# S5 layers on four quarters of the TensorE array, and the first layer's rotation tables from ScalarE sines

## The chip, the core and the metric

The kernel runs on one core of one Trainium2 chip. A core has engines that run side by side and are ordered only by semaphores: TensorE (PE in the profile; its weight loads are PEld), VectorE (DVE), ScalarE (ACT), GpSimd (POOL) and SyncE (SP), which issues transfers; ScalarE and POOL issue transfers too, each from its own queue. The metric is the device time of one execution in microseconds, median of the runs; lower is better.

## The reference

A trunk of four pre-norm residual layers over 256 positions of width 1024, one sequence. Layer i has the mixer i mod 3, so layers 0 and 3 are S5, layer 1 is forgetting attention, layer 2 gated linear attention. Every layer then has a squared-ReLU MLP (width 4096) and a gated per-layer input. What the change touches is the S5 mixer:

```python
def s5_mixer(xn, w_in, lam_re, lam_im, log_dt, b_re, b_im, c_re, c_im, d_skip, w_glu, w_out):
    u = xn @ w_in                                   # 64 groups of 16 channels, 64 states each
    dt = exp(log_dt)[:, None]
    mag = exp(lam_re * dt)
    ab_re, ab_im = mag * cos(lam_im * dt), mag * sin(lam_im * dt)
    ...                                             # bbar = coef(ab, lam) * b
    # per chunk: x = u . bbar (complex); s_t = ab * s_(t-1) + x_t; y = Re(s . c)
    ...
    y = y + d_skip * u
    z1, z2 = split(gelu(y) @ w_glu, 2)
    return (z1 * sigmoid(z2)) @ w_out
...
for i in range(DEPTH):
    h = h + mixer_i(rmsnorm(h, norm_mix[i]))
    h = h + square(relu(rmsnorm(h, norm_mlp[i]) @ mlp_w1[i])) @ mlp_w2[i]
    h = h + (p[i] @ ple_proj[i]) * sigmoid(rmsnorm(h, norm_ple[i]) @ ple_gate[i])
return rmsnorm(h, final_norm)
```

## The kernel before

Activations are kept transposed (channels on partitions, time along the row) in four tiles of 128 x 2 x 256. Large weights come in units of 256 x 512 (512 KB) through three `raw` buffers; ScalarE rounds each unit to a high part (`whi`, line 182), VectorE forms the rest (`wlo`, line 184), and TensorE does three (or, for the wide MLP products, effectively one and a half) passes with them. This is the work of most of the span.

An S5 layer is cut into four blocks b = 0 to 3 of 16 groups. A block's 16 groups stand as 8 pairs p; pair member g = 0 or 1 lies on the lower or the upper 64 partitions. Time is cut into 64 steps of 4 positions: the way in gathers 4 positions x 16 channels = 64 rows into 64 states, a scan runs over the 64 steps, and the outputs take 64 states back to 4 x 16 rows. A complex state is turned by a rotation table (`rot`, 128 x 8 x 2 x 64) so that the scan has a real factor only, and turned back behind it.

The work is written as steps with one letter and the block's number, and two orders by hand, `FIRST` for layer 0 and `LATER` for layer 3, say in which order the steps are traced. The tile framework then orders each engine's instructions by that priority and by when it expects them to be ready; in layer 3 TensorE's order is pinned to the traced one, and a short head of layer 0 (up to `u0`) is pinned on ScalarE, TensorE and, at its end, VectorE. The steps that matter here:

- `w` / `u`: half a block of the dense input product (line 1241), then its scaling by the row scale (line 1247) and eight small transfers that gather `U` (line 1075, four from SP's queue, four from ScalarE's). `z0`, `z1`: the row scale (POOL's power, line 365; TensorE and ScalarE, lines 375 and 377).
- `f`: loads of the way-in weights; in layer 0 of their parts, and `i` forms them on VectorE (lines 968 to 970); in layer 3 of the finished weights (one buffer, `win`) and the finished rotation table.
- `r`: block b's rotation table in layer 0, on VectorE: two products of 128 x 1024 (line 990) and two sums of 128 x 512 (lines 992, 993) from `F1` and `F8`, tables of powers that `s5_scalars` forms at the start with some fifty short complex products (lines 879 to 903, helper lines 783 to 785). `rot` for block 0 is begun in the head, between `z1` and `u0`.
- `o`, `k`: output weights (lines 1008 to 1012) and the short-range kernel (lines 1033 to 1044), which goes through memory into `tm` (line 1052).
- `x`: the way in, on TensorE (line 1087). `s`: states on VectorE (two products of 128 x 1024 at line 1097, two sums at 1098 and 1099, two scans at 1102). `e`: turned back (lines 1112 to 1121). `y`: outputs on TensorE (line 1133), Gelu on ScalarE (line 1142). `t`, `g`: transposed and split (lines 1149, 1150, 1313).
- `P`, `p`: the layer's input projection (line 470). `d`, `l`: loads and splits of gate weights (the second half of `w_glu`), `a`, `b`: the gate products for them (lines 201 to 203). These are dense work put between the S5 steps.

In layers 0 to 2, `s5_ahead` prepares layer 3's tables a little at a time behind the MLP and leaves them in memory (`kept`).

The way in and the outputs work on 64 x 64 pieces, and both pair members stay on their own half of the array:

```python
for g in range(2):
    r = slice(g * 64, (g + 1) * 64)
    matmul(px[r, p, :], w[r, p], U[r, p, :], ...)   # rows of half g, columns of half g
```

PSUM tiles come from tags: `wk` (3 buffers), `acc` (3), `mk` (1) and `po` (1); the outputs of a block go to `mk`, the transposes of `t` to `po`, which `g` reads.

Of the kernel before, what the change touches and what calls it, by code (L numbers as in the profile page):

```python
# [9 lines left out]
F32 = mybir.dt.float32  # L10
# [12 lines left out]
        "acc": 3, "wk": 3, "po": 1, "mk": 1}  # L23
# [37 lines left out]
class Trunk:  # L61


    def __init__(self, ctx, tc, A):
# [45 lines left out]
        nc.gpsimd.memset(self.halfpi, math.pi / 2)  # L110
        self.tms = [const(f"tm{i}", [P, 8, 4, 16]) for i in range(3)]
# [680 lines left out]
    def s5_scalars(self, j, late=False):  # L792
# [81 lines left out]

        F1, by_pair = self.small("F1", [128, 2, 32, 8], bufs=1), self.small("F8", [128, 32, 2, 8], bufs=1)
# [27 lines left out]
        d = self.small("dd", [128, 8, 16], bufs=1)  # L903
        self.tc.keep_in_program_order(V.tensor_tensor(d, self.eye16.unsqueeze(1).broadcast_to([128, 8, 16]), sd.unsqueeze(2).broadcast_to([128, 8, 16]), ALU.mult))
        r4 = new("r4")
        tt(r4, mag, mag, ALU.mult)
        tt(r4, r4, r4, ALU.mult)
        q = dict(cpow=G, powers=F, r4=r4, F1=F1, F8=by_pair, d=d)
        return q

    def s5_table(self, j, F):
# [9 lines left out]
        tab = self.dram.tile([2, 4, 4, 2, 8, 64], F32, name=f"tab{j}")  # L921
        for i in range(2):
            for g in range(2):
                nc.gpsimd.dma_start(tab[g, :, :, i].rearrange("s b p n -> (s b) p n"), ct[:, i, g, :])
        return tab

    def s5_spread(self, b):

        out = []
        for i in range(2):  # L930
            ps = self.psum()
            for p in range(8):
                for g in range(2):
                    self.last_mm = self.nc.tensor.matmul(ps[g * 64:(g + 1) * 64, p * 64:(p + 1) * 64], self.pick[:, p], self.ct[:, i, g, :], start=True, stop=True, skip_group_check=True)
            out.append(ps)
        return out
# [8 lines left out]
    def s5_fetch_in(self, j, b, pin=lambda x: x):  # L945
        bT = self.t4("bT", (128, 2, 512), tag="wt")
        pin(self.nc.gpsimd.dma_start(bT, self.A["s5_bT"][j, b]))
        return bT

    def s5_fetch_powers(self, tab, b, pin=lambda x: x):  # L950
        cf = self.t4("coef", (128, 2, 512), tag="wt")
        for g in range(2):
            pin(self.nc.gpsimd.dma_start(cf[g * 64:(g + 1) * 64], tab[g, :, b].rearrange("s i p n -> s (i p n)").unsqueeze(0).broadcast_to([16, 4, 1024])))
        return cf
# [6 lines left out]
    def s5_in(self, b, bT, cf, ahead=False):  # L961

        nc = self.nc
        if not ahead:
            w = [self.wp.tile([128, 2, 8, 64], F32, name=n, tag=n, bufs=BUFS[n]) for n in ("wh", "wl")]
            f = [t.rearrange("x i p n -> x i (p n)") for t in w]
            re, im = cf
            nc.vector.tensor_tensor(f[0], bT, re.unsqueeze(1).broadcast_to([128, 2, 512]), ALU.mult)
# [4 lines left out]
        w = [self.flat(win[:, i]) for i in range(2)]  # L973
        t = self.scratch((2, 512))
        t = [t[:, i] for i in range(2)]
        self.two(w[0], bT[:, 0], cf[:, 0], bT[:, 1], cf[:, 1], ALU.subtract, t[0])
        yield
        self.two(w[1], bT[:, 0], cf[:, 1], bT[:, 1], cf[:, 0], ALU.add, t[1])
        self.keep(b, 0, win, ahead)

# [551 lines left out]
```

## Time and profile before

| | us |
|---|---|
| median of three runs | 1417.9 (1415.36 to 1418.76) |
| the profiled execution | 1413.62, its span 1411.9 |
| TensorE matmul busy | 1376.1 (97%) |
| TensorE weight loads busy | 1247.5 (88%) |
| VectorE busy | 1034.7 (73%) |
| ScalarE busy | 708.5 (50%) |
| GpSimd busy | 107.7 (8%) |
| granted TensorE clock, mean | 0.994 |

A row of busy time by stretch gives the stretch, its length, then each engine's busy time with its count of instructions, then the granted clock (PEclk, 1.00 is full), the share of the 16 DMA engines and GB/s. A row of the timeline gives the start, the time from the first start to the last end, the engine and line, the operation, output<-inputs, the shape, the count, and in brackets the idle time in front with what ended it. A row of a group gives, behind the bar, the busy time, the mean duration of one in ns, and the idle time in front. Matmuls are pipelined, so each one's duration is longer than the distance between two starts.

### The profile page before, as it was taken

How to read it: one execution, taken by the hardware profiler on the slowest of the kernel's cores; microseconds unless marked ns; L12 is line 12 of the kernel's file. 1: busy time of each engine (PE TensorE's matmuls, PEld its weight loads, DVE VectorE, ACT ScalarE, POOL GpSimd, SP SyncE). 2: the span in 40 equal slices, each digit the busy share in tenths (PEclk: the TensorE clock that was granted, in tenths of full speed). 3: DMA queues.
4: the chain of work that ended last, by engine and by line, in shares of the span. 5: the costliest groups of instructions: out<-in, count | busy, mean ns of one | idle time of the engine just before them, and what ended most of it. 6: DMA issues, size and time to landing. Idle time of an engine off the chain costs nothing.

```text
span 1411.9 us, 26657 instructions
## 1 busy us (share of the span) xinstructions
PE 1376.1 (97%) x10794; PEld 1247.5 (88%) x10794; DVE 1034.7 (73%) x1638; ACT 708.5 (50%) x1110; POOL 107.7 (8%) x179
## 2 busy tenths in 40 slices
PE   9898999999999999999999999999999999999997
PEld 8788988889999978888988698888998899888897
DVE  9985678776867678897676568888666857766764
ACT  3234565454645565455566355555452355545553
POOL 3000000010110000110005100100004100000020
PEclk9999999999999999999999999999999999999999
DMA  9434656657554446776665356666666455556551
GB/s 306 128 114 124 182 176 196 184 182 234 181 149 138 133 136 209 249 232 206 183 187 148 107 162 195 212 206 220 203 207 204 164 195 172 187 167 212 188 180 60
DMA packets 144475, 254.80 MB, mean 180 GB/s; under 512 B 22192, under 2 KB 33552, under 8 KB 144352
## 3 DMA queue, kind: packets, MB, share of 16 engines
q1 hardware_dynamic: 130336, 227.80, 51.9%
q0 software_dynamic: 7744, 23.73, 4.9%
q10 hardware_dynamic: 6272, 1.58, 0.5%
q8 instruction: 84, 1.38, 0.4%
q14 instruction: 39, 0.32, 0.1%
HBM read 242.81 MB, written 8.13 MB: 178 GB/s over the span
## 4 chain that ended last, share of the span: by engine, by line
PE 65%; ACT 1%; DVE 1%; issue 1%; POOL 1%; DMA 1%; DVEq 0%; POOLq 0%; ACTq 0%; SPq 0%
PE wk L237 9%; PE acc L237 7%; PE wk L239 5%; PE acc L239 4%; PE acc L201 3%; PE wk L201 3%; PE wk L202 3%; PE wk L203 3%; PE acc L202 3%; PE acc L203 3%; PE mk L237 3%; PE po L237 2%; PE acc L1241 2%; PE mk L239 1%; PE acc L264 1%; PE acc L265 1%
## 5 line engine op out<-in xcount | busy, mean ns | idle before, releaser
L184 DVE TENSOR_TENSOR wlo<-raw,whi 128x1024 fp32r<-128x1024 f32 x396 | 482.5, 1226 | 270.5 <-ACT whi L182 266.2
L182 ACT CAST whi<-raw 128x1024 fp32r<-128x1024 f32 x396 | 412.5, 1049 | 484.3 <-PE po L237 73.8
L237 PE MATMUL wk<-x,whi 128*128 128x512 f32 x576 | 181.7, 396 | 0.8 <-DVE relu L248 0.8
L239 PEld LDWEIGHTS wk<-x,wlo 128*128 128x128 f32 x576 | 107.1, 188 | 23.6
L237 PE MATMUL acc<-s,whi 128*128 128x512 f32 x384 | 119.7, 395 | 0.0
L239 PE MATMUL wk<-x,wlo 128*128 128x256 f32 x576 | 113.4, 279 | 0.0
L237 PEld LDWEIGHTS wk<-x,whi 128*128 128x128 f32 x576 | 89.8, 189 | 2.5 <-DVE relu L248 0.8
L239 PEld LDWEIGHTS acc<-s,wlo 128*128 128x128 f32 x384 | 71.4, 188 | 16.5
L201 PE MATMUL acc<-x,whi 128*128 128x256 f32 x288 | 81.6, 287 | 0.9 <-ACT pp L456 0.9
L203 PE MATMUL acc<-x,wlo 128*128 128x256 f32 x288 | 82.1, 286 | 0.2 <-DVE wlo L184 0.2
L202 PE MATMUL acc<-x,whi 128*128 128x256 f32 x288 | 81.8, 285 | 0.0
L237 PE MATMUL mk<-x,whi 128*128 128x512 f32 x256 | 81.6, 395 | 0.0
L239 PE MATMUL acc<-s,wlo 128*128 128x256 f32 x384 | 76.0, 280 | 0.0
L203 PE MATMUL wk<-s,wlo 128*128 128x256 f32 x256 | 72.4, 283 | 0.0
L202 PE MATMUL wk<-s,whi 128*128 128x256 f32 x256 | 72.4, 283 | 0.0
L201 PE MATMUL wk<-s,whi 128*128 128x256 f32 x256 | 72.4, 283 | 0.0
L237 PE MATMUL po<-s,whi 128*128 128x512 f32 x192 | 60.3, 395 | 0.0
L237 PE MATMUL wk<-s,whi 128*128 128x512 f32 x192 | 59.5, 395 | 0.0
L237 PEld LDWEIGHTS acc<-s,whi 128*128 128x128 f32 x384 | 58.9, 189 | 0.6
L237 PE MATMUL acc<-x,whi 128*128 128x512 f32 x192 | 58.8, 396 | 0.0
L239 PEld LDWEIGHTS mk<-x,wlo 128*128 128x128 f32 x256 | 47.6, 188 | 10.3
L201 PEld LDWEIGHTS acc<-x,whi 128*128 128x128 f32 x288 | 54.7, 191 | 1.9 <-ACT pp L456 1.1
(413 smaller groups left out, 3382.6 us busy)
## 6 DMA issues: line engine op xcount, KB each, us to landing
raw<-mlp_w SPq DMA_DIRECT2D x256, 512.0 KB, 3.8
raw<-s_w_glu SPq DMA_DIRECT2D x32, 512.0 KB, 4.5
raw<-ple_gate SPq DMA_DIRECT2D x32, 512.0 KB, 3.6
raw<-fox_w_in SPq DMA_DIRECT2D x24, 512.0 KB, 3.8
raw<-gla_w_in SPq DMA_DIRECT2D x24, 512.0 KB, 3.7
raw<-s_w_out SPq DMA_DIRECT2D x16, 512.0 KB, 3.6
kept<-kept POOLq DMA_DIRECT2D x12, 512.0 KB, 5.3
raw<-ple_proj SPq DMA_DIRECT2D x8, 512.0 KB
```

What stands on the lines that cost most here:

```text
L182: nc.scalar.copy(hi, raw)
L184: self.last_lo = nc.vector.tensor_tensor(lo, raw, hi.bitcast(F32), ALU.subtract)
L201: mm(ps, hi, x[:, 0], start=first, stop=False, skip_group_check=True)
L202: mm(ps, hi, x[:, 1], start=False, stop=False, skip_group_check=True)
L203: self.last_mm = mm(ps, lo, x[:, 0], start=False, stop=last, skip_group_check=True)
L237: mm(ps[n], hi[:, i, s], v[i], start=first and i == 0, stop=False, skip_group_check=True)
L239: self.last_mm = mm(ps[n][:, 0], lo[:, i, s], v[i][:, 0], start=False, stop=last and i == UK - 1, skip_group_check=True)
L264: mm(ps[half], a[:, 0, t], hi[:, k], start=k0 + k == 0, stop=False)
L265: mm(ps[half], a[:, 0, t], lo[:, k], start=False, stop=False)
L1241: self.last_mm = nc.tensor.matmul(ps[:, n], raw[:, k, c], x[4 * i + k], start=i == k == n == 0, stop=i == 1 and k == 3, skip_group_check=True)
```

## The change

Five things are changed.

1. **Four quarters.** The host turns the data so that for pairs 4 to 7 the two members' states stand on the opposite half from their inputs. In the way in, pairs 0 to 3 (h = 0) go from rows of half g to columns of half g, pairs 4 to 7 (h = 1) from rows of half g to columns of half 1 - g, each h into a PSUM tile of its own; four matmuls on four different quarters are issued in turn. The outputs go back likewise, into two PSUM tiles (`mk` and `po`), and Gelu is taken in two halves. The states work on halves: one product of 128 x 1024 and two sums of 128 x 256 for each h.
2. **Copies of U.** For the outputs' short-range part of pairs 4 to 7, ScalarE copies that half of U to the other 64 partitions (`s5_inputs_turned`, in step `e`), pinned behind the previous block's Gelu.
3. **Rotation tables of layer 0.** `s5_scalars` forms, in place of the power tables, angles in half turns (`s5_steps`, a dozen VectorE operations, three of 128 x 512); `r` adds two of them on VectorE, takes an absolute value and two sines on ScalarE, one product on VectorE, and a square and an affine on ScalarE (`s5_turns`). Layer 3's tables, made ahead, keep the old form (`s5_circle`).
4. **Orders.** `r1` moves behind `s0`, `r2` and `r3` in front of `y0`, `i1` behind `y0`; block 0's table is whole before `u0`. In `LATER`, the way-in weights have a step `F` of their own, early, in the four-buffer tag `wt`; `x2`, `u3`, `x3`, `a0` move forward, `g1` and `g2` back; `t0` stands inside `w7`.
5. **Transfers.** The coefficient loads of a block are four instead of two, of half the size.

```diff
+        "v1": 2, "acc": 3, "wk": 3, "po": 1, "mk": 1}
-FIRST = """i0 w2 w3 r0 x0 f2 w4 o0 j2 P0 s0 k0 w5 u1 w6 d0 e0 y0 r1 i1 f3 x1 t0 o1 j3 k1 g0 u2 w7 l0 P1 d1 s1 a0 p0 e1 y1 r2 i2 x2 t1 o2 k2 g1 u3 p1 p2 d2 p3 d3 l1 b0 l2 d4 a1
-d5 s2 e2 y2 l3 b1 r3 i3 x3 t2 o3 k3 g2 l4 d6 a2 l5 d7 b2 s3 e3 y3 l6 l7 t3 g3 a3 b3"""
-LATER = """D0 D2 D1 D3 c0 w0 w2 n0 z0 f0 q0 w1 z1 D4 D5 u0 w3 P0 u1 w4 D6 D7 d0 x0 s0 w5 d1 f1 q1 x1 e0 w6 y0 u2 s1 w7 t0 l0 g0 f2 x2 u3 P1 e1 q2 y1 l1 d2
-s2 p0 p1 t1 g1 f3 x3 q3 p2 e2 y2 p3 d3 s3 a0 t2 g2 l2 d4 b0 l3 d5 a1 e3 l4 d6 b1 l5 d7 y3 a2 l6 t3 b2 l7 g3 a3 b3"""
+FIRST = """i0 w2 w3 x0 f2 w4 o0 j2 P0 s0 r1 k0 w5 u1 w6 d0 e0 r2 r3 y0 i1 f3 x1 t0 o1 j3 k1 g0 u2 w7 l0 P1 d1 s1 a0 p0 e1 y1 i2 x2 t1 o2 k2 g1 u3 p1 p2 d2 p3 d3 l1 b0 l2 d4 a1
+d5 s2 e2 y2 l3 b1 i3 x3 t2 o3 k3 g2 l4 d6 a2 l5 d7 b2 s3 e3 y3 l6 l7 t3 g3 a3 b3"""
+LATER = """D0 D2 D1 D3 c0 w0 w2 n0 F0 z0 f0 q0 F1 w1 z1 D4 D5 u0 w3 P0 u1 w4 F2 F3 D6 D7 d0 x0 s0 w5 d1 f1 q1 x1 u2 e0 w6 y0 s1 v7 f2 x2 u3 l0 g0 P1 e1 q2 y1 l1 d2
+s2 p0 f3 x3 t1 p1 q3 a0 e2 y2 p2 d3 g1 s3 l2 p3 t2 d4 b0 l3 d5 a1 g2 e3 l4 d6 b1 l5 d7 y3 a2 l6 t3 b2 l7 g3 a3 b3"""
...
+        self.steps = const("steps", [P, 2, 8])
+        for k in range(8):
+            for i in range(2):
+                nc.gpsimd.memset(self.steps[:, i, k:k + 1], float(k + 1 - i))
...
+    def s5_turns(self, q, b):
+        rot = self.t4("rot", (128, 8, 2, 64), tag="m4")
+        y = self.scratch((2, 8, 64))
+        one, eight = (q["turns"][:, i, b * 8:b * 8 + 8] for i in range(2))
+        nc.vector.tensor_tensor(y[:, 0].rearrange("x p (a b) -> x p a b", b=8), eight.unsqueeze(3).broadcast_to([128, 8, 8, 8]),
+                                one.unsqueeze(2).broadcast_to([128, 8, 8, 8]), ALU.add)
+        nc.scalar.activation(y[:, 1], y[:, 0], AF.Abs)
+        s, c = rot[:, :, 1], rot[:, :, 0]
+        nc.scalar.activation(s, y[:, 0], AF.Sin, scale=math.pi)
+        nc.scalar.activation(c, y[:, 1], AF.Sin, scale=-math.pi, bias=self.halfpi)
+        nc.vector.scalar_tensor_tensor(c, s, 2.0, c, ALU.mult, ALU.mult)
+        nc.scalar.activation(s, s, AF.Square, scale=math.sqrt(2.0))
+        nc.scalar.activation(s, s, AF.Identity, scale=-1.0, bias=1.0)
+        return rot
...
+    def s5_inputs_turned(self, U):
+        V = self.t2("V", (128, 4, 64), tag="v1")
+        for g in range(2):
+            self.nc.scalar.copy(V[g * 64:(g + 1) * 64], U[(1 - g) * 64:(2 - g) * 64, 4:8])
+        return U, V
+
     def s5_way_in(self, U, win):
-        xs = []
+        xs = [self.psum((128, 2, 4, 64)) for _ in range(2)]
+        gs = [slice(g * 64, (g + 1) * 64) for g in range(2)]
         for ri in range(2):
-            px = self.psum((128, 8, 64))
-            for p in range(8):
+            for p in range(4):
                 for i, w in enumerate(win[ri]):
-                    for g in range(2):
-                        r = slice(g * 64, (g + 1) * 64)
-                        self.nc.tensor.matmul(px[r, p, :], w[r, p], U[r, p, :], start=i == 0, stop=i == len(win[ri]) - 1, skip_group_check=True)
-            xs.append(px)
+                    for h in range(2):
+                        for g in range(2):
+                            self.nc.tensor.matmul(xs[h][gs[g ^ h], ri, p], w[gs[g], 4 * h + p], U[gs[g], 4 * h + p], start=i == 0,
+                                                  stop=i == len(win[ri]) - 1, skip_group_check=True)
         return xs
...
-            V.tensor_tensor(t, px.unsqueeze(2).broadcast_to([128, 8, 2, 64]), rot, ALU.mult)
-        V.tensor_tensor(R[:, 0], X[:, :, 1], Y[:, :, 0], ALU.add)
-        V.tensor_tensor(R[:, 1], X[:, :, 0], Y[:, :, 1], ALU.subtract)
+        for h, (t, px) in enumerate(zip((P, W), xs)):
+            p = slice(4 * h, 4 * h + 4)
+            t = self.flat(t).rearrange("x (r p i j) -> x r p i j", r=2, p=4, i=2)
+            V.tensor_tensor(t, px.unsqueeze(3).broadcast_to([128, 2, 4, 2, 64]), rot[:, p].unsqueeze(1).broadcast_to([128, 2, 4, 2, 64]), ALU.mult)
+            V.tensor_tensor(R[:, 0, p], t[:, 0, :, 1], t[:, 1, :, 0], ALU.add)
+            V.tensor_tensor(R[:, 1, p], t[:, 0, :, 0], t[:, 1, :, 1], ALU.subtract)
...
-        py = self.psum((128, 8, 64), "mk")
+        py = [self.psum((128, 4, 64), tag) for tag in ("mk", "po")]
...
+        for n in range(-1, len(parts)):
+            for p in range(4):
+                for h in range(2):
+                    for g in range(2):
+                        q, r = 4 * h + p, gs[g ^ h]
+                        x, w = (us[h][r, p], tm[r, q]) if n < 0 else (parts[n][0][r, q], parts[n][1][r, :, q])
+                        nc.tensor.matmul(py[h][gs[g], p, :], x, w, start=n < 0 and p == 0, stop=n + 1 == len(parts) and p == 3, skip_group_check=True)
-        self.last_gelu = nc.scalar.activation(G, py.rearrange("x p (i c) -> x i p c", i=4), AF.Gelu_apprx_tanh)
+        for h in range(2):
+            self.last_gelu = nc.scalar.activation(G[:, :, 4 * h:4 * h + 4], py[h].rearrange("x p (i c) -> x i p c", i=4), AF.Gelu_apprx_tanh)
...
         def r(b):
-            rots[b] = drain(self.s5_rot(q, b) if b else rot), decay(b)
+            rots[b] = self.s5_turns(q, b), decay(b)
...
         def e(b):
+            with self.tc.issue_after(self.last_gelu.ins) if b else nullcontext():
+                us[b] = self.s5_inputs_turned(us[b])
             states[b] = self.s5_turned(*states[b], rots[b][0], first)
...
                 with self.in_order(mybir.EngineType.DVE):
                     z(1)
-                    rot = self.s5_rot(q, 0)
-                    next(rot)
+                    r(0)
                     f(0)
                     v["mm"] = self.last_mm
                     v["u"] = u(0)
```

More of the change, by code (lines that the diff above doesn't have):

```diff
@@ L873, in s5_scalars, with s5_circle @@
         yield
+        rots = {}
+        if late:
+            yield from self.s5_circle(rots, sn, cs, t, cmul)
+        else:
+            rots["turns"] = self.s5_steps(th, k, t)
+        d = self.small("dd", [128, 8, 16], bufs=1)
+        self.tc.keep_in_program_order(V.tensor_tensor(d, self.eye16.unsqueeze(1).broadcast_to([128, 8, 16]), sd.unsqueeze(2).broadcast_to([128, 8, 16]), ALU.mult))
+        r4 = new("r4")
+        tt(r4, mag, mag, ALU.mult)
+        tt(r4, r4, r4, ALU.mult)
+        return dict(cpow=G, powers=F, r4=r4, d=d, **rots)
+    def s5_circle(self, rots, sn, cs, t, cmul):
+        nc = self.nc
+        V, tt = nc.vector, nc.vector.tensor_tensor
+        new = lambda name: self.small(name, [128, 32], bufs=1)
         F1, by_pair = self.small("F1", [128, 2, 32, 8], bufs=1), self.small("F8", [128, 32, 2, 8], bufs=1)
@@ L1269, in f, with F @@
                 cf = self.s5_fetch_powers(self.tab, b, self.tc.keep_in_program_order) if b else None
[L1270 removed]
+                parts[b] = bT, cf if b else self.s5_spread(b)
             else:
[L1272 to L1273 removed]
                 rots[b] = fetch(b, 1, (128, 8, 2, 64), "m4"), decay(b)
+        def F(b):
+            win = fetch(b, 0, (128, 2, 8, 64), "wt")
+            ins[b] = [[win[:, i]] for i in range(2)]
         def j_(b):
```

88 lines of the change are left out of this document (47 added, 41 removed).

## The prediction

> **What bounds the kernel now.** I read the page first, then the busy time by stretch, then the timeline of each engine in the two stretches that hold an S5 layer (layer 0 from the start to 123.70 us, layer 3 from 1055 to 1136 us).
>
> ```profile
> span 1411.9 us, 26657 instructions
> PE 1376.1 (97%) x10794; PEld 1247.5 (88%) x10794; DVE 1034.7 (73%) x1638; ACT 708.5 (50%) x1110; POOL 107.7 (8%) x179
> core 0: us, PE busy (x) PEld busy (x) DVE busy (x) ACT busy (x) POOL busy (x), PEclk, DMA share, GB/s
> 400.00:700.00 300.00, 294.85 (x1994) 265.38 (x1995) 227.56 (x380) 164.81 (x280) 11.82 (x23) 1.00 0.59 183
> 21.91:114.48 92.57, 84.19 (x1451) 76.67 (x1447) 85.67 (x102) 25.15 (x52) 6.54 (x14) 0.98 0.49 146
> 114.48:123.70 9.22, 7.24 (x177) 6.51 (x175) 0.74 (x2) 3.42 (x5) 0.00 (x0) 1.00 0.07 11
> 1077.90:1121.87 43.97, 40.65 (x638) 36.08 (x634) 43.07 (x51) 12.32 (x20) 11.80 (x21) 1.00 0.60 196
> 1121.87:1132.50 10.63, 10.63 (x161) 10.43 (x160) 5.23 (x5) 2.48 (x3) 0.00 (x0) 1.00 0.59 199
> ```
>
> Outside S5 TensorE is the bound (294.85 of 300 us in 400 to 700), and the change does not touch those layers, so what S5 gains reaches the end. Inside S5 two engines are full together: in layer 0 VectorE is busy 85.67 of 92.57 us and TensorE 84.19; in layer 3 VectorE 43.07 of 43.97, and behind it TensorE has 10.63 us of 10.63 left to do. Taking work from one of the two alone would move little; the change takes from both in layer 0, from TensorE alone in layer 3.
>
> **The quarter matmuls.** In the two stretches the way in (line 1087) and the outputs (line 1133) issue 512 + 640 small matmuls in layer 0 and 256 + 384 in layer 3:
>
> ```profile
> 0.00:185.00 185.00, 16.32 (x512) 15.69 (x512) 0.99 0.55 170
> 1040.00:1160.00 120.00, 9.62 (x256) 8.38 (x256) 1.00 0.60 196
> 0.00:185.00 185.00, 21.57 (x640) 20.87 (x640) 0.99 0.55 170
> 1040.00:1160.00 120.00, 12.01 (x384) 11.52 (x384) 1.00 0.60 196
> 1076.72 2.08 PE L1087 MATMUL wk<-U,kept 64*64 64x64 f32 x64
> 1078.73 3.72 PE L1241 MATMUL acc<-x,wl 128*128 128x256 f32 x16
> 1084.65 2.08 PE L1087 MATMUL wk<-U,kept 64*64 64x64 f32 x64 [2.20 <-issue]
> 37.10 0.65 PE L1033 MATMUL mk<-qo,bx 128*32 128x64 f32 x32
> 37.69 0.26 PE L1036 MATMUL mk<-dd,ident 32*32 32x32 f32 x8
> ```
>
> From start to next start, 64 of them take 2.01 us, 31.4 ns each. A whole-array f32 matmul of 256 columns takes 228 ns (the sixteen of line 1241 end 3.72 us after they begin, the last one's drain of some 0.07 included), so 64 columns alone are 57 ns: the two diagonal quarters run side by side, the other two stand idle. The change gives pairs 4 to 7 to the two idle quarters, and issues the four in turn. Nothing in this trace uses two row halves on one column half. The nearest row with four parts at work is line 1033 (four column strips, same 64 columns): 32 in 0.59 us, 18.4 ns each. Bounds: 31.4 (the two new quarters take turns with the old) and 57/4 = 14 (perfect). I take 18.4, since that row has four streams and its own start and end in it: 13.0 ns saved, 15.0 us over 1152 in layer 0, 8.3 us over 640 in layer 3, as TensorE content, not yet as time.
>
> The Trainium skill, page TensorE: Matmul & The Clock Gate, Part 1 ("Wait — 56ns, not 53.3ns?"), states that start to start never falls below about 25 ns; by that the 13.0 ns would be 6.4, and the two contents 7.4 and 4.1 us. The row of 18.4 ns on this chip is below that floor, so I do not use it. The page TensorEngine Tiling (Array Packing), Gotcha 1, says that different row tiles cannot access one PSUM bank simultaneously, which would forbid the new form, as each bank keeps both row halves; but the pairs of today write one bank from both halves at 31.4 ns, so for separate partitions the trace does not agree.
>
> **Rotation tables, layer 0.** VectorE builds them now from products; these groups are those of 19.5 to 115 us:
>
> ```profile
> L990 DVE TENSOR_TENSOR rot<-F,F 128x1024 f32<-128x1024 f32 x4 | 4.8, 1212 | 0.0
> L992 DVE TENSOR_TENSOR rot<-rot,scratch 128x512 f32<-128x512 f32 x4 | 2.7, 686 | 0.1
> L1098 DVE TENSOR_TENSOR R<-P,W 128x512 f32<-128x512 f32 x4 | 2.7, 682 | 0.0
> L783 DVE TENSOR_TENSOR F<-F 128x128 f32<-128x128 f32 x2 | 0.6, 282 | 0.0
> L184 DVE TENSOR_TENSOR wlo<-raw,whi 128x1024 fp32r<-128x1024 f32 x8 | 9.8, 1219 | 3.9 <-ACT whi L182 3.9
> L1142 ACT ACTIVATE G<-mk 128x512 f32<-128x512 f32 x4 | 2.4, 598 | 11.2 <-PE mk L1133 11.2
> L1142 ACT ACT_TABLE_LOAD x1 | 1.3, 1283 | 0.0
> 22.81 1.21 DVE L990 TENSOR_TENSOR rot<-F,F 128x1024 f32<-128x1024 f32 x1
> 23.95 0.68 DVE L992 TENSOR_TENSOR rot<-rot,scratch 128x512 f32<-128x512 f32 x1
> 24.54 0.68 DVE L993 TENSOR_TENSOR rot<-rot,scratch 128x512 f32<-128x512 f32 x1
> ```
>
> By start to next start a 1024-element operation occupies VectorE 1.14 us and a 512-element one 0.60. A block's table costs two of each, 3.48 us; after, one add and one product of 512, 1.20. For blocks 1 to 3 that is 6.8 us off. Of block 0 the three rows from 22.81 (2.3 us) leave the time after the first u. In each block's states two 512-element sums become four of 256, put halfway between 0.28 and 0.68, with 0.34 to the next: 1.36 for 1.20, 0.6 us over four blocks. VectorE's 85.67 us after 21.91 become 85.67 - 6.8 - 2.3 + 0.6 = 77.2.
>
> ScalarE gains five 512-element operations a block (0.6 each, 12 us), two copies of U's upper half a block and a second Gelu half; it is busy 25.15 of 92.57, so I cost these at nothing except where VectorE waits for the sines. If that cover is gone, they cost up to the 12. The Sine table is loaded in the head already; blocks 1 to 3 ask for sines ahead of the first Gelu, so no load is added if they stay there (1.28 us each otherwise).
>
> **The head.** Here the order is pinned:
>
> ```profile
> 19.05 0.28 DVE L904 TENSOR_TENSOR dd<-eye,sd 128x128 f32<-128x128 f32 x1
> 19.78 0.70 PE L375 MATMUL wk<-diag,ones 128*128 128x256 f32 x2
> 20.52 0.37 ACT L377 COPY rstd<-wk 128x256 f32<-128x256 f32 x1 [6.12 <-PE wk L375]
> 21.91 1.06 DVE L1247 TENSOR_TENSOR u<-acc,rstd 128x512 f32<-128x512 f32 x1
> ```
>
> The some fifty short products that VectorE works through until 19.05 become a dozen operations, but this brings nothing: the row scale waits for TensorE at 19.78, behind its dense matmuls. It costs: block 0's table is now traced between z1 and u0, so on ScalarE its absolute value and two sines queue behind the copy of rstd (end 20.89; about 0.55 each, to 22.6), and on VectorE the product of 0.6 stands ahead of u0. So u0 comes at 23.2 for 21.91, 1.3 us late. Four of its eight U transfers leave from ScalarE's queue, now also behind a square, an affine and block 0's decay; x0 is late by those 1.3 us and up to 2 more, while VectorE has the way-in and way-out weights of block 0 to form. On POOL, 16 small fills come into the head and four coefficient transfers for two into each block; POOL is busy 6.54 of 92.57 us, and I cost them at nothing. In layer 3 the first load of way-in weights passes POOL's power for the row scale; it is one issue, made while TensorE still runs the layer before.
>
> The copies of U's upper half wait, on ScalarE, for the previous block's Gelu; behind them stand the casts that feed VectorE's wlo, and the outputs wait for them. Both Gelu and U come well before the outputs' last input from VectorE, so this too is nothing while ScalarE keeps to a third of its time.
>
> **Sum, layer 0.** Today the last VectorE step of block 3 ends at 114.48, 6.9 us of VectorE idle included. From 23.2 with 77.2 us of work it ends at 100.4 with no idle, 107.3 with all of it. I take half, 103.9, since of that idle only the 3.9 us on ScalarE's casts has no reason to shrink: 10.6 us earlier (7.2 to 14.1). TensorE's content of 91.4 between 21.91 and 123.70 falls to 76.4, so it is not the limit. Then comes the tail:
>
> ```profile
> 116.08 1.15 PE L1133 MATMUL mk<-tm,U 64*64 64x64 f32 x32 [0.62 <-DMA tm<-lags]
> 122.98 0.39 PE L201 MATMUL acc<-g,whi 128*128 128x256 f32 x1 [0.68 <-ACT g L1150]
> 50.15:53.56 3.41, 1.31 (x43) 1.17 (x40) 3.41 (x5) 0.00 (x0) 0.00 (x0) 1.00 0.66 184
> 53.56:56.97 3.41, 3.41 (x71) 3.41 (x68) 1.98 (x2) 2.33 (x2) 0.00 (x0) 0.50 0.00 1
> ```
>
> Its 8.5 us to the gate matmuls at 122.98 lose the 1.6 us wait for tm (started after o3, which no longer trails) and 160 x 13 ns = 2.1 us, and gain 0.3 for the second Gelu: 3.4. Against it stands the clock: where TensorE was busy 1.31 of 3.41 us, the next 3.41 ran at 0.50. With more TensorE idle I allow one more such stretch, 1.7 us. Layer 0: 10.6 + 3.4 - 1.7 = 12.3.
>
> **Sum, layer 3.** VectorE's chain is not shortened (+0.6), so TensorE's 8.3 us count only as far as it trails:
>
> ```profile
> 1109.95 0.67 DVE L1121 TENSOR_TENSOR P<-P,W 128x504 f32<-128x504 f32 x1
> 1110.73 1.99 PE L470 MATMUL wk<-praw,raw 128*128 128x256 f32 x8
> 1118.43 0.12 PE acc L202
> 1121.19 0.68 DVE L1121 TENSOR_TENSOR P<-P,W 128x504 f32<-128x504 f32 x1
> 1129.47 1.15 PE L1133 MATMUL mk<-tm,U 64*64 64x64 f32 x32
> ```
>
> The last outputs start 7.6 us after VectorE has given them their input, so TensorE trails. Walking the new order: the outputs of block 2 need e2, which ends at 1110.6 today and some 0.5 later with the split sums, and bank po, which g1, traced after them, must free first (0.6 us of VectorE): they start near 1112 and last 96 x 18.4 ns = 1.8. Behind them, ahead of block 3's outputs, stand two projections (eight matmuls, 1.9 each), the turn (0.5) and three gates (24 x 0.12 = 2.9 each; today one projection and four gates): TensorE comes to about 1126.9 for 1129.47, and the outputs' own 96 are 1.2 us shorter: 3.8. The way-in weights, in one buffer now (the 2.20 us wait above is for that load), move to a pool of four and are loaded ahead; the idle that this removes is in front of e2 and so in the walk already. Bounds: 0 (TensorE waits for VectorE instead) and 8.3.
>
> Together 12.3 + 3.8 = 16.1 us. The profiled execution took 1413.62 us round its span of 1411.9; it lies 4.3 below the median of 1417.9. 1413.62 - 16.1 = 1397.5, on the scale of the median 1401.8; I say 1402.
>
> **Rivals.** More gain (8%): layer 0 keeps no VectorE idle, layer 3 gives its whole content: 14.1 + 3.4 + 7.5 = 25, 1393. Sines late (15%): the tables' one scratch buffer is held through three ScalarE operations, so r2 and r3 queue, and a Gelu may fall between sines (two loads of 1.28 each time); half of layer 0's gain goes, 8 to 10 us remain, 1409. For it: that buffer and VectorE's 3.9 us waits on ScalarE copies; against: ScalarE's low share. Quarters in turn (12%): 31.4 ns stays; layer 0 is then bound by TensorE's 91.4 us plus half of today's 10.4 us of waiting, 5 us gained, layer 3 about 1: 1412. For it: no row shows two row halves on one column half. Slower (5%): the clock gate. Each closed 3.41 us costs 1.7; ten more of them cancel the gain and thirteen make it slower, 1423. Against: TensorE would still be 76.4 of some 87 us busy in layer 0, far over the 38% that closed it.
>
> **Numbers.** Forecast 60%, own range 1395 to 1408. The range to 1392 and 1411 takes in the first rival and the sines. 0.3% (4.25 us) is about what a measurement here tells from no change, the line is 1413.6. Faster: 60 + 8 + 13 + 5 = 86%; same 9% (most of the rest of quarters in turn and of the sines); slower 5%.
>
> **What would show it.** Small matmuls at 14 to 18 ns in four starts close together, else the quarters failed. Block 3's last VectorE step near 104, the first gate matmul behind the last turn near 111. No Sine table load after the first Gelu. In layer 3, counted from its first way-in (1076.72 now), block 3's outputs start 50 us on, not 52.75, with no wait of 2.2 us at the second way-in. Wrong it would be if granted clock in layer 0 falls under 0.9, or VectorE idles over 7 us on ScalarE.

## The result and the profile after

| | before | after |
|---|---|---|
| median, us | 1417.59 (6 runs, 1415.36 to 1418.76) | 1427.69 (6 runs, 1423.46 to 1428.14) |
| profiled execution, its span | 1413.62, 1411.9 | 1427.7, 1425.7 |
| granted clock, mean | 0.994 | 0.983 |

The ratio is 1.0068 [1.0056, 1.0080]: 10 us slower, where 16 us faster was forecast. The two profiled spans lie 13.8 us apart; some 4 of it are scatter, since the execution profiled before was a quick one. The head of the page, and the stretches that answer to those of before (layer 0 from u0 to the last VectorE step of block 3, the tail to the first gate matmul behind the last turn, layer 3 from u0 to the first states, and from there to the last VectorE step; columns as in the prediction):

```profile
span 1425.7 us, 26727 instructions
PE 1363.9 (96%) x10794; PEld 1233.1 (86%) x10794; DVE 1023.6 (72%) x1610; ACT 726.6 (51%) x1154; POOL 115.6 (8%) x207
22.67:119.89 97.22, 74.59 (x1414) 66.05 (x1413) 78.91 (x102) 37.83 (x80) 8.50 (x17) 0.90 0.51 142
119.89:127.28 7.39, 5.97 (x187) 5.46 (x186) 0.03 (x1) 3.07 (x6) 0.00 (x0) 0.97 0.02 4
1075.94:1090.53 14.59, 8.92 (x94) 7.47 (x93) 2.11 (x3) 0.62 (x1) 8.26 (x15) 0.86 1.02 334
1090.53:1134.78 44.25, 36.21 (x609) 30.61 (x606) 43.87 (x59) 15.00 (x30) 3.38 (x6) 0.93 0.36 104
```

TensorE and VectorE both do less, as forecast (12.2 and 11.1 us less over the span), and both take longer. In layer 0 VectorE's work fell from 85.67 to 78.91 us and the stretch grew from 92.57 to 97.22: its idle time went from 6.9 to 18.3 us. The first gate matmul behind the last turn came at 127.28 for 122.98: layer 0 lost 4.3 us between these two profiles. That figure is loose, since the layer varies from execution to execution: two kernels below, e1 and e5, have the same layer 0, and its last split on VectorE (`g3`) starts at 128.21 and 121.23 there, for 127.25 here. Layer 3 lost more, before its first states: 14.59 us from u0, where the kernel before had 7.6 (1070.32 to 1077.91).

**The small matmuls** became shorter by about as much as forecast (way in, line 1148, and outputs, line 1200; each for 0 to 185 and 1040 to 1160 us; 16.32, 9.62, 21.57 and 12.01 before):

```profile
0.00:185.00 185.00, 12.28 (x512) 11.28 (x512) 0.94 0.57 168
1040.00:1160.00 120.00, 6.75 (x256) 5.62 (x256) 0.96 0.59 186
0.00:185.00 185.00, 11.13 (x640) 10.17 (x640) 0.94 0.57 168
1040.00:1160.00 120.00, 7.62 (x384) 6.71 (x384) 0.96 0.59 186
```

14.5 us less in layer 0 (15.0 forecast) and 7.3 in layer 3 (8.3). In layer 0 two misses cancel in that sum: an output takes 17.4 ns and a way-in matmul 24.0, where 18.4 was taken for both. The first block's 128 way-in matmuls ran mostly at half clock and alone are busy for 4.12 us; the fourth block's, at full clock, for 2.35. The question is where the saved time went.

**Layer 3: U comes late.** VectorE's timeline has nothing between these two rows but the second u:

```profile
1075.94 1.06 DVE L1308 TENSOR_TENSOR u<-acc,rstd 128x512 f32<-128x512 f32 x1 [2.84 <-ACT rstd L381]
1090.53 1.23 DVE L1159 TENSOR_TENSOR P<-wk,kept 128x1024 f32<-128x1024 f32 x1 [10.49 <-PE wk L1148]
```

GpSimd's timeline (`kept` are loads of 512 KB, `tm` smaller ones), and after it a step of the chain of work (start, us, what):

```profile
1075.87 1.61 POOL L1276 DMA_DIRECT2D kept<-kept  x3
1078.06 1.05 POOL L1276 DMA_DIRECT2D kept<-kept  x2 [0.58 <-DMA tm<-kept]
1079.10 1.71 POOL L1106 DMA_DIRECT2D tm<-kept  x3
```

```profile
1080.65 8.42 DMA U<-u
```

U0's eight transfers of 32 KB begin at 1077.02. Around them GpSimd issues five loads of 512 KB (F1 to F3 and two of block 1's); the DMA engines are busy 1.02 of the stretch at 334 GB/s, and the chain stands 8.42 us on U. 2.6 MB at 334 GB/s are 7.8 us. The list of transfers gives U's eight (count, size, median us from issue to landing), here from 1072 to 1083 and then in the kernel before from 1066 to 1078, with U1 among them:

```profile
U<-u SPq DMA_DIRECT2D x4, 32.0 KB, 7.8
U<-u ACTq DMA_DIRECT2D x4, 32.0 KB, 9.4
```

```profile
U<-u SPq DMA_DIRECT2D x8, 32.0 KB, 2.7
U<-u ACTq DMA_DIRECT2D x8, 32.0 KB, 2.7
```

In the kernel before, the loads' queue stood still at that time (its timeline):

```profile
1068.53 2.32 POOL L1052 DMA_DIRECT2D tm<-kept  x4
1079.11 1.64 POOL L1215 DMA_DIRECT2D kept<-kept  x3 [8.26 <-PE wk L1087]
```

Block 1's load into the one buffer had to wait until the first way-in had read it, and everything behind it on the queue waited too. The small buffer was a throttle; four buffers took it away.

**Layer 0: three kinds of new idle time.** VectorE's waits from 20 to 120 us (what waited for what: us in total, times, longest):

```profile
DVE wlo L188 <- ACT whi L186: 9.6, 5, 5.1
DVE rot L1030 <- ACT rot L1029: 7.3, 2, 4.0
DVE P L1159 <- PE wk L1148: 4.1, 1, 4.1
```

TensorE's from 20 to 130 us, six of its eight rows (`issue` is time in which the profile shows nothing that it waited for):

```profile
PE acc L206 <- DVE P L1172: 8.0, 2, 5.5
PE wk L1148 <- DMA U<-u: 4.8, 2, 3.5
PE mk L1200 <- issue: 1.5, 1, 1.5
PE wk L1148 <- issue: 1.5, 1, 1.5
PE po L1200 <- issue: 1.4, 1, 1.4
PE mk L1087 <- issue: 1.4, 1, 1.4
```

VectorE's first row is not ScalarE being slow: it is what ended the time in which VectorE had nothing to do until the next way-in (5.1 us before block 3's states, where ScalarE itself had first waited for TensorE's gate matmuls; see e7). In the second, 4.0 us lie in the head ahead of u0 and 3.4 on block 3's sine. TensorE's last four rows, 5.7 us, are new (0.4 before); the last section looks at where they stand.

### The profile page after: what moved, and what is told of

Same layout as the page of the kernel before. It is cut to its first block, busy times and chain, and to the rows that moved or that the text cites. A ratio compares the mean times of both kernels' runs of the same rounds, so it can differ in the third digit from the quotient of the medians.

```text
span 1425.7 us, 26727 instructions
## 1 busy us (share of the span) xinstructions
PE 1363.9 (96%) x10794; PEld 1233.1 (86%) x10794; DVE 1023.6 (72%) x1610; ACT 726.6 (51%) x1154; POOL 115.6 (8%) x207
## 3 DMA queue, kind: packets, MB, share of 16 engines
q8 instruction: 84, 1.38, 0.4%
## 4 chain that ended last, share of the span: by engine, by line
PE 60%; DVE 4%; ACT 2%; DMA 1%; issue 1%; SPq 0%; DVEq 0%; POOLq 0%; ACTq 0%
PE wk L241 9%; PE acc L241 7%; PE wk L243 5%; PE acc L243 4%; PE wk L205 3%; PE wk L206 3%; PE wk L207 3%; PE acc L205 3%; PE acc L206 3%; PE acc L207 3%; PE mk L241 3%; PE po L241 2%; PE mk L243 1%; PE acc L268 1%; PE acc L269 1%; PE acc L270 1%
## 5 line engine op out<-in xcount | busy, mean ns | idle before, releaser
L243 PEld LDWEIGHTS acc<-s,wlo 128*128 128x128 f32 x384 | 71.5, 188 | 16.5
```

Source lines behind the costliest of these rows:

```text
L243: self.last_mm = mm(ps[n][:, 0], lo[:, i, s], v[i][:, 0], start=False, stop=last and i == UK - 1, skip_group_check=True)
```

## Experiments

Theories: A, U comes late because large loads run beside it. B, the sines cost more through ScalarE than they save. C, the steps' order no longer fits. D, TensorE runs out of instructions. All times are medians; the ratio is to the kernel before. "Below" and "above" compare medians of separate rounds, in which the kernel before itself moved between 1416.9 and 1418.3; by the intervals such a difference is good to 2 to 3 us.

**e1, one buffer again in layer 3**

```diff
-            win = fetch(b, 0, (128, 2, 8, 64), "wt")
+            win = fetch(b, 0, (128, 2, 8, 64), "win")
-n0 F0 z0 f0 q0 F1 w1 ... F2 F3 D6 ... f1 q1 ... f2 x2 ... f3 x3
+n0 z0 F0 f0 q0 w1 ... D6 ... F1 f1 q1 ... F2 f2 x2 ... F3 f3 x3
```

> The changed kernel with one part undone: in layer 3 the way-in weights go back into one buffer and are loaded where the block's rotation table is loaded, instead of early into a pool of four. Theory A (U comes late): the early loads run beside the small U transfers; in the changed kernel the first product of block 0's states starts 14.6 us behind u0 in layer 3, in the kernel before 7.6 us. A expects that distance back at 7 to 9 us and the time 5 to 8 us below the changed kernel. Rival B (sines): nothing in layer 3 has to do with it, 0. Rival C (order of the steps, quarters themselves): the distance stays over 12 us, 0.

1421.37 us, 1.0029 [1.0015, 1.0043]: 6.3 below the changed kernel. Block 0's states start 7.65 us behind u0. The fourth way-in now waits 5.1 us for its loads (U behind the weights that had to wait for the buffer).

**e2, products in layer 0.** The old tables and the old order of layer 0, all else as changed.

```diff
-            rots[b] = self.s5_turns(q, b), decay(b)
+            rots[b] = drain(self.s5_rot(q, b) if b else rot), decay(b)
```

> The changed kernel with the rotation tables of layer 0 formed on VectorE from products again, in the old order of layer 0, so that four quarters, copies of U, the four coefficient loads and all of layer 3 stay. Rival B (the sines' chain through ScalarE and one scratch buffer is what costs): layer 0 ends 8 to 12 us sooner than in the changed kernel, since the quarters then gain what they were to gain. A (late U): of the 3.2 us that U comes later in layer 0, the 2 us of ScalarE's queue go, and 6.8 us more VectorE work comes back: between 3 us faster and 3 us slower. C (step order on VectorE): the order is the old one, so the 5.5 us wait of TensorE near 74 us goes, 4 to 8 us faster.

1422.08 us, 1.0030 [1.0016, 1.0044]: 5.6 below, within C's 4 to 8 and short of B's 8. In the profile, TensorE's longest wait for the turned states went from 5.5 to 2.5 us. VectorE has 86.4 us of work from u0 to its last step, 7.5 more than in the changed kernel, and still ends 1.1 us sooner (118.78 for 119.89): its idle time falls from 18.3 to 10.4. So more work for VectorE, in its old order, did not make layer 0 longer. This edit undoes the sines and the new order together; no run has the sines in the old order.

**e3, U's transfers in front of the rest of block 0's table** (a `yield` ahead of the square, resumed behind `u(0)`).

> The changed kernel, only the last part of block 0's table (the square, the affine and the decay on ScalarE) is traced behind the U transfers instead of in front. A: ScalarE's four U transfers leave 2 us sooner, s0 comes 1 to 3 us sooner, and the time falls by 1 to 3 us. B and C: s0 waits for other things, less than 1 us.

1424.14 us, 1.0057 [1.0035, 1.0079]: 3.5 below, but with e11 it did not come again.

**e4, two coefficient loads.** Left out is the exchange of halves for pairs 4 to 7.

```diff
-        for g in range(2):
-            for h in range(2):
-                ... tab[g ^ h, :, b, h] ... [16, 4, 512]
+        for g in range(2):
+            ... tab[g, :, b] ... [16, 4, 1024]
```

> The changed kernel with the coefficients of a block loaded by two transfers with rows of 4 KB as before, instead of four with rows of 2 KB; what is left out is the exchange of the halves for pairs 4 to 7. A, if the number and size of the rows is what crowds U out in layer 0: U0 lands 2 to 4 us sooner and the time falls by 2 to 4 us. If it is the bytes alone: under 1 us.

1424.48 us, 1.0049 [1.0031, 1.0066]: 3.2 below, against medians whose runs spread over 5 to 7 us; no more than a hint.

**e5, loads of layer 3 held until U is there**

```diff
+            if b > 1:
+                keep(nc.gpsimd.tensor_copy(win[:, 0, 6:8, 0:1], us[b - 2][:, 6:8, 0:1]))
-n0 F0 z0 f0 q0 F1 w1 ... F2 F3 D6 ... f1 q1 ... f2 x2
+n0 F0 F1 z0 f0 q0 w1 ... D6 ... F2 f1 q1 ... F3 f2 x2
```

> The changed kernel, way-in weights of layer 3 in the four-buffer pool as there, but the loads of blocks 2 and 3 wait on GpSimd until the last two pieces of U0 and U1 have landed (a copy of 128 x 2 elements from U into the buffer stands in front of the load, and holds the loads behind it on that queue too), and those of blocks 0 and 1 stand in front of the row scale. A (late U): block 0's states start 7 to 9 us behind u0 in layer 3 for 14.6 in the changed kernel, and the 5.1 us that TensorE waited for the fourth way-in with one buffer do not come back: 6 to 11 us faster than the changed kernel. If only the bytes in all matter and not when they are loaded: over 12 us behind u0, under 2 us faster.

1417.45 us, 1.0007 [0.9996, 1.0019]: 10.2 below the changed kernel, level with the kernel before. GpSimd's timeline, then VectorE's:

```profile
1076.72 0.18 POOL L1338 COPY kept<-U 128x2 f32<-128x2 f32 x1 [6.21 <-DMA U<-u]
1077.22 0.56 POOL L1339 DMA_DIRECT2D kept<-kept  x1 [0.32 <-DMA U<-u]
```

```profile
1070.59 1.05 DVE L1308 TENSOR_TENSOR u<-acc,rstd 128x512 f32<-128x512 f32 x1 [2.86 <-ACT rstd L381]
1078.18 1.22 DVE L1159 TENSOR_TENSOR P<-wk,kept 128x1024 f32<-128x1024 f32 x1 [3.49 <-PE wk L1148]
```

The states start 7.59 us behind u0. From u0 to block 3's last turn (`g3`) layer 3 takes 67.7 us in this profile, 74.7 in the changed kernel and 66.8 before: the held loads account for 7 us. In every kernel with the early loads (the changed one, e2, e3, e4, e6 and e7) this stretch takes 73.7 to 74.7 us, in e5 and those built on it (e9 to e13, e15 to e17) 66.5 to 67.7. So A is shown for layer 3, and so is that the rest of the change gains nothing there. The other 3 us of the medians are not explained: layer 0 is the same code in both kernels, and its first gate matmul behind the last turn comes at 121.25 in this profile and at 127.28 in the changed kernel's.

**e6, the same matmuls, two quarters at a time** (the loop over h outermost in the way in and in each term of the outputs).

> The changed kernel with the same matmuls in another order: pairs 0 to 3 first, then pairs 4 to 7, so that two quarters at a time are busy as in the kernel before, not four. Theory D (supply of instructions): in the changed kernel a burst of four-quarter matmuls uses a packet of 256 TensorE instructions faster than the next one comes, which shows as idle time of TensorE put down to issue, 5.9 us in layer 0. D expects starts of about 31 ns apart, these gaps gone (under 1 us), so that a block's 160 outputs take 5.0 us for 3.8 to 4.0 now, and the time 0 to 5 us above the changed kernel. If the quarters' 15 us of content counted in full, 8 to 15 us above. If the gaps have another cause than the rate, they stay.

1430.02 us, 1.0091 [1.0074, 1.0108]: 2.3 above the changed kernel. The way in and the outputs of layer 0:

```profile
0.00:185.00 185.00, 17.66 (x512) 16.56 (x512) 0.94 0.55 165
0.00:185.00 185.00, 14.93 (x640) 13.85 (x640) 0.94 0.55 165
```

9.2 us of small matmuls more in layer 0 alone cost 2.3 us of time, a quarter of themselves; the two intervals allow anything from almost nothing to two thirds, but not the whole. The issue gaps did not go (4.9 us in three), against my expectation: the bursts still use 256 instructions in under 3 us (outputs 23 ns each).

**e7, i3 and x3 in front of l3 and b1**

> The changed kernel with i3 and x3 traced in front of l3 and b1 in layer 0. Theory C (steps in an order made for more VectorE work): VectorE runs out of work before block 3's states, 8.2 us idle between 97 and 108.5 us, since the fourth way-in stands behind 24 gate matmuls; C expects x3 3 us sooner and the time 2 to 5 us below the changed kernel. A and B: x3 waits for its U or its table, no change.

1426.65 us, 1.0063 [1.0047, 1.0079]: 1.0 below. The two stretches to the first gate matmul behind the last turn:

```profile
22.40:111.53 89.13, 70.47 (x1390) 61.07 (x1388) 76.80 (x101) 37.57 (x79) 8.53 (x17) 0.92 0.50 146
111.53:124.91 13.38, 10.17 (x208) 9.66 (x209) 1.75 (x3) 3.37 (x6) 0.00 (x0) 0.87 0.19 54
```

C was half right: VectorE ended 8.1 us sooner (89.13 for 97.22; part of that may be chance, as e5 with the old order shows 92.38), and the tail grew by 6.0 (13.38 for 7.39), since TensorE still had the gate matmuls to do in front of the outputs.

**e8, the sines alone on the kernel before** (with the new order of layer 0).

> The kernel before with the sines in place of the products and the new order of layer 0, without quarters, copies of U, four coefficient loads and without any change in layer 3. My sum would give 6 to 9 us faster than the kernel before (9.1 us less VectorE work). B (the sines' chain costs more than it brings) and C (the saved work turns into VectorE idle time): 0 to 5 us slower than the kernel before, with over 15 us of VectorE idle time in layer 0 for 6.9.

1431.30 us, 1.0092 [1.0075, 1.0109]: 14.4 slower than the kernel before, more than B and C allowed. VectorE's waits from 23 to 126 us:

```profile
DVE wlo L188 <- ACT whi L186: 12.1, 5, 5.3
DVE rot L1028 <- ACT rot L1027: 9.4, 2, 5.5
DVE P L1149 <- PE wk L1139: 3.4, 1, 3.4
DVE qo L1060 <- PE mk L1185: 2.5, 1, 2.5
```

From u0 on VectorE has 7.7 us less to do, and 24 us of idle time for 6.9 (4.0 us of the second row lie ahead of u0).

**e9 to e12, on e5.** e9 puts the products and the old order of layer 0 back; e10 gives the angles tiles of their own (`y = [self.a2(...) for i in range(2)]`); e11 is e3's edit; e12 is e10 and e11 together.

> e5 (loads of layer 3 held) with the products and the old order of layer 0 from e2: the quarters without the sines. If what e2 and e5 brought adds (5.6 and 10.2 us below the changed kernel), 1412 us, 5 below the kernel before: then the quarters by themselves gain, and the sines take 5 us from it. If the quarters gain nothing in layer 0 and the sines were free: 1417, as e5.

> e5 with two tiles of their own (128 x 512 each, from a pool of four) for the angles of the sines, in place of the one scratch buffer that they share with the output weights. B1 (that buffer is what makes the sines late: VectorE stands 3.2 us on a sine near 54 us and the next output weights wait behind it): that wait goes, 2 to 5 us below e5. If ScalarE's queue is what is late (B2): the wait stays and the time within 1.5 us of e5.

> e5 with the square, the affine and the decay of block 0 behind the U transfers (e3). If e3's 3.5 us add: 1414. If they were the scatter of the head's transfers: within 1.5 us of e5.

> e5 with both edits of e10 and e11. If both costs are real and apart, 1410 to 1413; if the sines are late for another reason (ScalarE's queue behind the U and tm transfers and behind the copies of U), 1415 to 1418.

e9 1416.68, 0.9985 [0.9974, 0.9997]; e10 1422.29, 1.0025 [1.0011, 1.0039]; e11 1418.27, 1.0002 [0.9993, 1.0011]; e12 1415.33, 0.9990 [0.9976, 1.0005]. Beside the quarters, sines and products come out alike (e5 0.8 above e9), each with its own order of layer 0. The one scratch buffer, a rival of the prediction, was there (VectorE's wait of 3.2 us on a sine near 54 us is gone in e10 and e12), but the time rose by 4.8 in e10 and fell by 2.1 in e12; ScalarE's queue (e11) brought nothing. These edits do not add.

**e13, e14 and e16, block 2's loads in layer 0 held until U0 is there,** on e12, on the kernel before and on e9; **e15,** e13 with r2 and r3 in front of u1.

```diff
+        if behind is not None:
+            pin(nc.gpsimd.tensor_copy(bT[:, 0, 6:8, 0:1], behind[:, 6:8, 0:1]))
```

> e12 with the loads of block 2 in layer 0 (way-in parts, coefficients and what follows on GpSimd's queue) held until the last pieces of U0 have landed, by the same small copy as in layer 3. If the late U costs in layer 0 as well: the first way-in ends 2 to 5 us sooner (block 0's states start 12 to 14 us behind u0 for 15.6) and the time is 2 to 5 us below e12's 1415.3. If layer 0 is bound elsewhere: within 1.5 us of e12.

> The kernel before, only with the loads of block 2 in layer 0 held until the last pieces of U0 have landed. If U0's landing sets layer 0: 2 to 4 us below the kernel before. If VectorE's work sets it (85.7 of 92.6 us busy): 0 to 1.5 us.

> e13 with the tables of blocks 2 and 3 traced right behind block 1's, in front of u1, so that their sines stand in front of the U transfers of block 1 on ScalarE's queue. If the sines' place on that queue costs: 2 to 5 us below e13. If not, or if work that was beside other work now stands ahead of u1: 0 to 4 us above.

> e9 (quarters, products, loads of layer 3 held) with the loads of block 2 in layer 0 held too. If the late U costs in layer 0: 2 to 5 us below e9's 1416.7, and below the kernel before beyond doubt. If e16 and e13 come out alike within 2 us, the sines bring nothing that the products did not.

e13 1416.44, 0.9993 [0.9982, 1.0005]; e14 1421.61, 1.0031 [1.0018, 1.0045]; e15 1415.88, 0.9988 [0.9977, 0.9998]; e16 1417.39, 1.0007 [0.9996, 1.0017]. Nothing is gained, and the kernel before loses 4 us. In e13 and e14 the edit did not bring block 0's states nearer to u0 (e13 16.5 us for 15.6 in e12; e14 13.6, as in the kernel before), so block 2's loads do not seem to be what makes U0 late there; in e16 it did (14.8 for 18.9 in e9), and the time stayed. Nor is the edit only a delay: the small copy, 0.2 to 0.4 us in layer 3 of e5, takes GpSimd 0.86 us here in e13, 5.26 in e14 and 3.42 in e16. The waits suggest, without showing it, that the held loads meet the next small transfers. TensorE's longest wait on a transfer, of e14 and then of e13:

```profile
PE mk L1135 <- DMA U<-u: 6.2, 1, 6.2
```

```profile
PE mk L1203 <- DMA tm<-lags: 4.7, 1, 4.7
```

**e17, dense work sooner, on e12; e18, the same order on the kernel before.**

```diff
-x1 t0 ... s1 a0 p0 e1 ... u3 p1 p2 ... y2 l3 b1 i3 x3 t2
+x1 p0 p1 t0 ... s1 a0 e1 ... u3 p2 ... y2 i3 x3 l3 b1 t2
```

> e12 with three edits of layer 0's order: p0 and p1 (sixteen dense matmuls, 3.7 us of TensorE) directly behind x1, where TensorE stands 5 to 8 us before the first gates, and i3 x3 in front of l3 b1. If TensorE's work after 95 us is what keeps the gain back: 3 to 6 us below e12's 1415.3. If the gaps in front of the gates are only moved: within 1.5 us of e12.

> The kernel before with the same edits of layer 0's order as e17 and nothing else. There VectorE is busy 93% of layer 0, so TensorE's order should matter less: within 2 us of the kernel before. If it gains as much as e17 does on e12, the order alone brings it, not the quarters.

e17 1423.85, 1.0039 [1.0023, 1.0054]; e18 1423.73, 1.0042 [1.0029, 1.0055]. Both are slower, by 8.5 and 5.5 us, so my last explanation fell. What they show is how much the order of layer 0 is worth by itself: a few steps moved cost the kernel before as much as half of the whole change.

## Why the prediction was wrong

- **Quarters and VectorE's work, right as content.** Small matmuls are 14.5 and 7.3 us shorter (15.0 and 8.3), VectorE has 78.9 us of work after u0 (77.2), u0 comes at 22.67 (23.2).
- **The step that failed in layer 3:** "they are loaded ahead; the idle that this removes is in front of e2 and so in the walk already". I gave the loads a place in the order and no price. They cost 7 us on U (shown by e1 and e5). I had quoted the 2.2 us wait for the one buffer as a cost only, and not asked what it held back. The Trainium skill, page DMA: Bandwidth & Descriptors, section Issuing engines are not separate DMA queues, says that transfers started by different engines run on the same 16 DMA engines and interleave. The trace agrees: U, from SP's and ScalarE's queues, stood 8.42 us beside loads from GpSimd's. The same page of the Trainium skill, section Rules for kernel authors, advises to issue a transfer early so that its setup overlaps with computing; here early loads made the small transfers late, and the 7 us of layer 3 (10.2 of the medians) went when the loads were held (e5).
- **The other term of layer 3,** 3.8 us less trailing, did not come even with e5: VectorE's stretch is 43.96 us as before, and the outputs of block 3 start 7.7 us behind it (7.6 before). TensorE's 7.3 us ran out in waits (7.8 us in e5 from 1070 to 1130, 3.2 before) and in two stretches of 3.41 us at half clock (none before). The step of the walk that failed is the wait for the outputs' second bank, which `g` must free first, and for which I had allowed 0.6 us. Block 1's outputs waited 2.5 us for it in e5 (first row). For block 2's, the step `e2` ended at 1110.7, about as forecast, but VectorE did block 3's first products and sums before `g1` (second row), and the outputs on that bank came right behind it, at 1115.6 (third row), where the walk had 1112. The releaser that the third row names is a short fill of VectorE's that ended beside `g1`.

```profile
PE po L1200 <- DVE g L1381: 2.5, 1, 2.5
1114.86 0.68 DVE L1381 TENSOR_TENSOR g<-po,g 128x512 fp32r<-128x512 f32 x1
1115.60 0.27 PE L1200 MATMUL po<-tm,V 64*64 64x64 f32 x2 [1.75 <-DVE P L1172]
```

- **The step that failed in layer 0:** "I take half" of 6.9 us as idle time. It was 18.3, and 13.9 and 19.7 in the profiles of e5 and e1 with the same layer 0. The bound "10.6 us earlier (7.2 to 14.1)" took VectorE's work as what sets the end. With 7.5 to 7.9 us of that work put back in its old order the time did not rise (e2 against the changed kernel, e9 against e5). With less work VectorE waited for the next way-in behind TensorE's gate matmuls (e7), and for ScalarE's sines, costed at nothing "except where VectorE waits for the sines": 3.4 us behind u0. Which of the waits sets the length of layer 0 is not shown.
- **The clock term** was mis-sized: one more stretch at half clock was allowed, five came. These are stretches of the changed kernel in layer 0, each with the 3.41 us in front of it:

```profile
31.57:34.98 3.41, 1.08 (x10) 0.64 (x10) 3.38 (x5) 0.22 (x1) 2.58 (x5) 1.00 1.00 260
34.98:41.81 6.83, 5.96 (x126) 5.43 (x127) 2.69 (x5) 2.79 (x6) 0.00 (x0) 0.50 0.72 189
69.12:72.53 3.41, 0.00 (x0) 0.00 (x0) 3.38 (x6) 0.00 (x0) 0.54 (x1) 1.00 0.33 96
72.53:79.36 6.83, 5.32 (x25) 5.09 (x27) 6.83 (x11) 0.00 (x0) 0.00 (x0) 0.50 0.52 125
110.08:113.49 3.41, 1.82 (x47) 1.25 (x45) 3.38 (x5) 2.62 (x7) 0.00 (x0) 1.00 0.52 159
113.49:120.32 6.83, 5.62 (x26) 5.63 (x27) 6.40 (x11) 0.74 (x1) 0.00 (x0) 0.50 0.41 110
```

  Each time TensorE had been busy at most 1.82 of 3.41 us. It then worked 16.9 us at half clock (3.4 before): 6.7 us more for the same matmuls. The rival "clock gate" had argued from TensorE's mean share; the clock goes by single stretches. From 20 to 126 us in all twenty profiles, cut at 3.41 us on the grid on which the clock changes, each of the 64 stretches at full clock with under 1.53 us of TensorE work was followed by half clock, 9 of the 24 with 1.53 to 1.85, and none of the 430 with more. With the 5.3 us more of issue gaps the half clock makes 12.0 of the 14.5 us that the quarters saved in layer 0. This is a sum of what the trace shows and not an experiment: no kernel kept the clock up with all else equal. It says where TensorE's saved time went, not what layer 0 lost, since TensorE's work counts there by a quarter or so (e6).
- **The sines:** no table load fell between them, and freeing the queue or the buffer brought nothing clear (e10, e11, e15). That sines and new order together lose 14.4 us on the kernel before, and 0.8 beside the quarters, is measured; how much of it is the order's, and why it fits the one and not the other, stays open.
- **The signs.** Of the two signs of being wrong that I had named, the clock came to the line (0.90 in layer 0), and 16.9 us of VectorE's idle time are put down to ScalarE, over the 7, though part of it began on TensorE. Block 3's last VectorE step came at 119.89, not near 104.

No version is clearly ahead: e9 and e15, the only ones whose interval lies below 1, are 0.15 and 0.12% below the kernel before, under the 0.3% that a forecast could claim.

## What to carry to other kernels

A single buffer that makes a load wait may be holding back a whole queue: before widening it, list what then runs beside the small transfers on the critical path, and hold those loads on the data that must land first. Work taken from two coupled engines is worth the time only where one of them sets the end; price a saved microsecond by undoing it (e6: about a quarter), and count idle time, half clock and issue gaps that the shorter bursts bring. An order written by hand fits one set of durations: a change of durations needs its own control with the order alone. Here e18 shows what an order can cost; the change's own new order was never run without the sines.

## What the hardware showed unexpectedly

TensorE stood in bursts of small matmuls at some of the places where its instructions pass a multiple of 256. One of the four gaps in layer 0 of the changed kernel, in TensorE's timeline, and the page's line of a transfer queue that carries instructions (packets, MB, share):

```profile
83.84 0.27 PE L1148 MATMUL wk<-U,wl 64*64 64x64 f32 x3 [1.46 <-issue]
```

```profile
q8 instruction: 84, 1.38, 0.4%
```

Numbering TensorE's instructions (matmuls, weight loads and its few waits) in the order of the trace, the four gaps stand in front of instructions 1218, 1985, 2241 and 2754, each 193 or 194 above a multiple of 256. Six more such places lie in small matmuls of that layer and show no gap; at three of them the last packet on that queue had started 11 to 16 us before. All 69 issue gaps over 0.35 us in layer 0 of the nineteen kernels other than the one before stand at such a number; they last 0.4 to 3.1 us (median 1.4) and end 2.2 to 3.2 us (median 2.4) behind the start of a packet of 16 KB on that queue. 1.38 MB in 84 packets are 16.4 KB each, and the 10794 matmuls with as many weight loads make 257 instructions for each packet. Four-quarter matmuls with their weight loads go through 256 instructions in about 2 us; the pairs of the kernel before took 4.0 (128 at 31.4 ns) and met one gap of 0.45, in two of the kernels built on it (e8, e14) one of 0.75 and 0.52. The Trainium skill, page Runtime: NRT & Kernel Launch, section Instruction fetch mechanics, says that instructions are refilled in blocks of 16 KiB, 256 of them, and that crossing a block is mostly hidden. The positions agree; that the cost is mostly hidden does not hold here, where the gaps are 5.7 us in one layer. The likely reading, which no run tests by itself, is that a burst which comes to the next 256 less than some 2 to 3 us after the packet's start has to wait for it.
